# A third Strassen product in a hybrid decoder layer, with three smaller moves in its order

## The chip, the cores and the metric

The kernel runs on one core of a Trainium2 chip. TensorE (PE) multiplies, VectorE (DVE) and ScalarE (ACT) do elementwise work, GpSimd (POOL) does a little elementwise work and issues stores, SyncE (SP) issues loads; 16 DMA engines move the data. Each engine takes its instructions in the order in which the program wrote them. The metric is the time of one execution on the device in microseconds (us), median of several runs.

## What is computed

One layer of a decoder, 1024 tokens by 1024 channels, all float32. Cut to what matters (`@` with weights is what PE does, the rest is elementwise):

```python
u = rms_norm(h, norm1_g)
z_pool, z_lru, z_gelu, z_gate = split(u @ w_in)            # 512, 1024, 1024, 2048 columns
y_pool = causal_multiscale_pool(z_pool, pool_w) @ pool_proj
y_lru  = rglru_branch(z_lru, z_gelu, ...) @ lru_proj        # conv, two gates per head, scan, gelu
gates  = sigmoid(z_gate + b_gate)
h = h + (gates[0] * y_pool + gates[1] * y_lru) @ w_out
v = rms_norm(h, norm2_g)
g, u = split(v @ w_ffn_in)                                  # 2 x 2816 columns
h = h + (silu(g) * u) @ w_ffn_out
h = h + sigmoid(rms_norm(h, ple_norm_g) @ w_ple_gate) * (p @ w_ple_proj)
out = rms_norm(h, final_g)
```

## The kernel before

Activations lie transposed: a tile is 128 channels (partitions) by 1024 tokens, 512 KB, and a low and a high half mean tokens 0 to 511 and 512 to 1023. To keep float32 precision each operand is split into a high part (a cast on ACT, `hi`, L113) and a low part (a subtraction on DVE, `lo`, L117), and each product takes three matmuls of 512 columns (`mm3`, L217 to L219; `mm6`, L225, is the same for a plain product over both halves).

The stages run one after the other: p @ w_ple_proj ("PLE", first), w_in, pool_proj, lru_proj, w_out, w_fin (w_ffn_in), w_fout (w_ffn_out), the gate of the PLE term, and the last norm. w_in, w_fin and w_fout use Strassen's algorithm (`strassen`), seven products where a plain one takes eight. A pair of weight tiles (A11 to A22) and a pair of activation tiles (B11 to B22) make 2x2 blocks. `PairOf` forms the sums of weights on DVE (L192). `Acts` forms the activation operands B11, T1, T2, B21, B22, T3, T4, with subtractions on DVE (L396 to L402) that overwrite their source tiles. A unit is one product q of one pair: 12 matmuls in one PSUM bank over four tile pairs. The products come in the order 1, 5, 6, 2, 3, 7, 4, and for each the two or three pairs of a group. `Plain` and `Gated` take a bank's content into the results (copies on ACT, additions on DVE), and the bank of a pair is kept over several products.

`drive` (L274) writes the order. For each unit it does the previous unit's rest (post), loads, casts and subtracts of the weights three ahead, the unit's own preparation, some steps of background work worth half the unit's time, and then the unit's matmuls. Background generators are a queue of which the first two are looked at; `yield None` means "not in this unit any more". Into that queue go the chains of the recurrence (`chain`, L614, with two gate products per head), pooling with its products, the softplus of the recurrence's parameter, and, in w_fin, the finished tiles' operands for w_fout, which are stored to DRAM (`hidden_ops`). Units that a generator puts into `inserted` are emitted before the next unit.

Around the change: w_lru's tiles come in `done_lru`, which multiplies by a gate, adds, and splits the tile (names g and m). w_out is a plain product (L225) over eight tiles. `done_out` adds it to x (tile xr, L898), stores h, adds h squared to ss (L324), and scales h in place by gain and reciprocal norm (L902). Operands of w_fin begin in it. w_fout runs in three chunks of 3, 4 and 4 tile pairs (`CHUNKS`), and each reads its seven kinds of operands back from DRAM: `Loaded.make` (L1009) issues all tiles of one kind at once, on SP, behind or ahead of weights (L146) as the program has them. `Residual` adds the chunks' banks to h (L1031) and, in the second, the stored h (tile hr, L1022).

## Time and profile before

| | us |
|---|---|
| runs, median of three | 1447.88 (1447.34 to 1450.69) |
| profiled execution | 1451.7 |
| its span, first to last instruction | 1450.0 |
| PE busy | 1383.5 (95%), 6006 matmuls |
| DVE busy | 1033.6 (71%) |
| ACT busy | 673.7 (46%) |
| POOL busy | 90.5 (6%) |
| granted TensorE clock, mean | 0.973 of full |

Busy time is time in which an engine executes; the rest is waiting. A matmul's end is modelled: one of 512 columns shows .39 us and issues every .23 us, so a busy PE can still be paced by its issue. Shares over the whole span mix stages with different limits, so a stage is read by its own window. A clock of 1.00 is 2.4 GHz, 0.50 is 1.2 GHz. In lists of waits "A <- B" says that A's engine sat idle until B ended.

### The profile page before, as it was taken

Reading aid. Unit: us, or ns where it says so; the run is one execution under the profiler, and the core shown is the slowest. Engines: PE = TensorE matmul, PEld = TensorE weight load, DVE = VectorE, ACT = ScalarE, POOL = GpSimd, SP = SyncE. Lnnn points to the kernel's source line nnn. Section 1 sums busy time; section 2 is a strip of 40 time slices with the busy share of each in tenths; the row PEclk is TensorE's granted clock in tenths of the full one; section 3 lists DMA queues with packets and bytes.
Section 4 is the critical chain, followed back from the end, with each engine's and each line's share of the span. In section 5 each row is a group of like instructions: output and inputs, shape, how many; then the busy total and the mean of one; then the engine's idle time right before and its main releaser. Section 6 shows DMA issues by size and latency. Waiting matters only on the chain.

```text
span 1450.0 us, 16454 instructions
## 1 busy us (share of the span) xinstructions
PE 1383.5 (95%) x6006; PEld 1133.5 (78%) x6006; DVE 1033.6 (71%) x1523; ACT 673.7 (46%) x1072; POOL 90.5 (6%) x194
## 2 busy tenths in 40 slices
PE   6899999999999999999899999999999889998986
PEld 4677887877887888888788888888888678886865
DVE  3887778778865454367798888888778667767465
ACT  5468584877876021223554444444444322235231
POOL 2200010010000000000001000101010100000000
PEclk8799999999999999999999999999999999999987
DMA  7222233332558323231124344344584997703203
GB/s 276 102 79 89 78 119 121 103 114 88 217 183 336 110 87 138 86 119 65 45 90 141 139 154 158 146 160 148 217 338 174 365 356 295 297 30 116 63 25 116
DMA packets 65025, 220.55 MB, mean 152 GB/s; under 512 B 7344, under 2 KB 9904, under 8 KB 64944
## 3 DMA queue, kind: packets, MB, share of 16 engines
q1 hardware_dynamic: 46224, 151.80, 29.7%
q0 software_dynamic: 18576, 67.64, 11.6%
q8 instruction: 47, 0.77, 0.2%
q14 instruction: 34, 0.28, 0.1%
q10 hardware_dynamic: 144, 0.06, 0.0%
HBM read 147.65 MB, written 71.83 MB: 151 GB/s over the span
## 4 chain that ended last, share of the span: by engine, by line
PE 58%; issue 8%; DVE 7%; DMA 3%; ACT 2%; POOL 0%; DVEq 0%; SPq 0%; POOLq 0%; ACTq 0%
PE ps L217 16%; PE ps L218 16%; PE ps L219 16%; PE ps L225 9%; DVE w L117 1%; DMA fT<-fT 1%; DMA fB<-fB 1%; DMA wr<-w_fout 1%; DVE wr L192 1%; PE ps L363 1%; DVE pg L1106 0%; ACT w L113 0%; ACT pg L1104 0%; DVE h L1107 0%; ACT sq L1112 0%
## 5 line engine op out<-in xcount | busy, mean ns | idle before, releaser
L113 ACT CAST w<-wr 128x512 fp32r<-128x512 f32 (+2 forms) x376 | 220.6, 608 | 339.3 <-DVE wr L192 179.4
L117 DVE TENSOR_TENSOR w<-wr,w 128x512 fp32r<-128x512 f32 (+2 forms) x376 | 250.1, 672 | 66.4 <-ACT w L113 64.7
L218 PE MATMUL ps<-xT,w 128*128 128x512 f32 x640 | 251.9, 394 | 5.6 <-DVE xT L117 5.6
L217 PE MATMUL ps<-xT,w 128*128 128x512 f32 x640 | 251.9, 394 | 4.6 <-DVE z L491 4.3
L219 PE MATMUL ps<-xT,w 128*128 128x512 f32 x640 | 251.2, 392 | 0.0
L218 PE MATMUL ps<-xB,w 128*128 128x512 f32 x480 | 188.4, 392 | 1.6 <-DVE xB L117 1.5
L217 PE MATMUL ps<-xB,w 128*128 128x512 f32 x480 | 187.8, 391 | 1.6 <-ACT xB L113 1.6
L219 PE MATMUL ps<-xB,w 128*128 128x512 f32 x480 | 187.8, 391 | 0.0
L218 PEld LDWEIGHTS ps<-xT,w 128*128 128x128 f32 x640 | 121.6, 190 | 31.9 <-DVE xT L117 6.8
L217 PEld LDWEIGHTS ps<-xT,w 128*128 128x128 f32 x640 | 121.5, 190 | 32.0 <-issue 3.5
L219 PEld LDWEIGHTS ps<-xT,w 128*128 128x128 f32 x640 | 121.6, 190 | 25.8 <-DVE w L117 0.2
L218 PEld LDWEIGHTS ps<-xB,w 128*128 128x128 f32 x480 | 90.7, 189 | 21.8 <-DVE xB L117 3.1
L217 PEld LDWEIGHTS ps<-xB,w 128*128 128x128 f32 x480 | 90.8, 189 | 21.2 <-ACT xB L113 2.0
L219 PEld LDWEIGHTS ps<-xB,w 128*128 128x128 f32 x480 | 90.8, 189 | 18.8
L225 PE MATMUL ps<-m,w 128*128 128x512 f32 x384 | 87.3, 389 | 0.0
L225 PE MATMUL ps<-y,w 128*128 128x512 f32 x384 | 87.2, 389 | 0.0
L217 PE MATMUL ps<-fT,w 128*128 128x512 f32 x176 | 71.0, 403 | 15.2 <-DVE h L1031 13.0
L225 PEld LDWEIGHTS ps<-y,w 128*128 128x128 f32 x384 | 72.1, 188 | 15.0
L225 PEld LDWEIGHTS ps<-m,w 128*128 128x128 f32 x384 | 72.0, 188 | 14.9
L1031 DVE TENSOR_TENSOR h<-h,ps 128x512 f32<-128x512 f32 x68 | 46.6, 685 | 39.8 <-PE ps L219 39.3
L192 DVE TENSOR_TENSOR wr<-wr 128x512 f32<-128x512 f32 (+1 forms) x104 | 70.5, 679 | 6.0 <-DMA wr<-w_fout 3.9
L218 PE MATMUL ps<-fT,w 128*128 128x512 f32 x176 | 70.2, 399 | 0.0
(209 smaller groups left out, 2200.7 us busy)
## 6 DMA issues: line engine op xcount, KB each, us to landing
wr<-w_fin SPq DMA_DIRECT2D x44, 512.0 KB, 5.6
fT<-xT POOLq DMA_DIRECT2D x44, 512.0 KB, 6.0
fT<-fT SPq DMA_DIRECT2D x44, 512.0 KB, 9.1
wr<-w_in SPq DMA_DIRECT2D x36, 512.0 KB, 4.0
fB<-xB POOLq DMA_DIRECT2D x33, 512.0 KB, 5.4
fB<-fB SPq DMA_DIRECT2D x33, 512.0 KB, 8.3
g<-z POOLq DMA_DIRECT2D x16, 512.0 KB, 3.9
g<-g SPq DMA_DIRECT2D x16, 512.0 KB, 5.6
```

The lines of the kernel that those rows point to most:

```text
L113: act.copy(op[:, :x.shape[1]], x)
L117: dve.tensor_tensor(op[:, H:H + n], x, op[:, :n].bitcast(F32), ALU.subtract)
L192: f(self.place(out), self.place(a), self.place(b))
L217: pe.matmul(bank, a, xop[:, :H], start=first, stop=False, skip_group_check=more)
L218: pe.matmul(bank, a, xop[:, H:], start=False, stop=False, skip_group_check=more)
L219: pe.matmul(bank, b, xop[:, :H], start=False, stop=last, skip_group_check=more)
L225: pe.matmul(bank, w, xop[:, s], start=f, stop=e)
L363: pe.matmul(bank[:, i * P:(i + 1) * P], r[:, b + i:b + i + 1].broadcast_to([P, P]), ident, start=True, stop=True)
L1031: dve.tensor_add(h[t][:, s], h[t][:, s], bank)
```

## The change

1. **w_out by Strassen.** `done_lru` no longer splits its tiles; neighbouring tiles (even a, odd b) are a pair of `ma`. For each pair a background generator (`some_operands`) makes B11, T1, T2 and B21; `prepare(ma)` makes what is left within w_out. w_out runs in two groups of two pairs. `Plain` collects each result in a tile z, and `residual` adds it to x, stores h, writes the scaled tile into its own tile v, and adds the square. The pairs of v are neighbours too, and the host puts the rows of w_out and w_fin in that order.
2. **Softplus** begins when the first group of w_in has its operands ("xa").
3. **Gate and pooling products** are put in after a `yield None`.
4. **The chunks' operands** are loaded one by one by `load_some`, which each unit of the chunk's first group and of the group before calls: from the fourth unit on (the first chunk from the fifth), one for each .8 units (1.1 in the first chunk). `hidden_ops` becomes `kept_operands`, and the wait for "va" moves to `Gated.last`.

```diff
@@ -455,6 +455,15 @@
             units.extend(unit(i + j, q, where, j, size) for q in QS for j in range(size))
             i += size
+    def some_operands(acts, k, names):
+        for name in names:
+            acts.run(name, k, 0)
+            yield {"T1": 0.7, "T2": 1.4, "T4": 0.7}.get(name, 0.1)
+            yield None
+            acts.run(name, k, 1)
+            yield 0.7
...
@@ -585,6 +594,8 @@
     e_, d_, s_, s2, acc, mx, nsp, psp = (sc[:, i, :] for i in range(8))
     def softplus():
+        while "xa" not in have:
+            yield None
         lam = cv[:, C_LAM:C_LAM + NH]
         act.activation(e_, lam, AF.Abs)
...
+    def kept_operands(a, b, out, k, key):
+        acts = Acts(1)
+        acts.a[0], acts.b[0] = a, b
+        for name in ORDER:
+            acts.run(name, 0, 0)
+            yield {"T1": 0.7, "T2": 1.4, "T4": 0.7}.get(name, 0.1)
+            yield None
+            acts.run(name, 0, 1)
+            store(out[name, k], acts.op.pop((name, 0)).bitcast(F32))
+            yield 0.7
+        have.add((key, k))
+    class Loaded:
+        def __init__(self, src, key, k0, n, order, begin, step):
+            self.src, self.key, self.k0, self.op = src, key, k0, {}
+            self.order, self.begin, self.step, self.units = order, begin, step, 0
+        def load_some(self, every=False):
+            n = len(self.order) if every else int((self.units - self.begin) / self.step) + 1
+            self.units += 1
+            for name, k in self.order[len(self.op):max(n, 0)]:
+                force((self.key, self.k0 + k))
+                self.op[name, k] = at("l" + name, F32R)
+                nc.sync.dma_start(self.op[name, k].bitcast(F32), self.src[name, self.k0 + k])
...
@@ -656,6 +695,7 @@
                 have.add(("rg", c, h))
             return Unit([], emit, post)
+        yield None
         inserted.append(half(0))
         yield None
         inserted.append(half(1))
@@ -732,8 +772,9 @@
             store(m_spill[gi], mx_)
             have.add(("mx", gi))
+        yield None
         inserted.append(Unit([], emit, post))
-        yield 0.5
+        yield 0.1
...
-    ms = {}
+    ma = Acts()
...
         for b, s in zip(banks, (LOW, HIGH)):
             dve.tensor_mul(g[:, s], g[:, s], b)
         dve.tensor_add(g, g, t0.pop(m))
-        ms[m] = split(g, "m")
+        if m % 2 == 0:
+            ma.a[m // 2] = g
+        else:
+            ma.b[m // 2] = g
+            background.append(some_operands(ma, m // 2, ORDER[:4]))
     plain([w_lru[m] for m in range(KD)], KD, lambda: ys, done_lru, pre_lru, 2)
...
-    def pre_out(m, a):
-        if a == 0:
-            if m == 0:
-                state["ss2"] = at("ss")
-                state["rep1"] = norm1.spread()
-                load_xr(0)
-            if m + 1 < KD:
-                load_xr(m + 1)
-    def done_out(m, banks):
-        h = xr.pop(m)
-        for b, s in zip(banks, (LOW, HIGH)):
-            dve.tensor_add(h[:, s], h[:, s], b)
-        store(h_spill[m], h)
-        add_square(h, state["ss2"], m == 0)
-        dve.scalar_tensor_tensor(h, h, col(C_G2, m), state["rep1"], ALU.mult, ALU.mult)
-        if m < 4:
-            va.a[m] = h
-        else:
-            va.b[m - 4] = h
-        if m == 3:
-            va.make("B11")
-        if m == 4:
-            va.make("T1")
-        if m >= 4:
-            va.run("T2", m - 4, 0)
-        if m >= 5:
-            va.run("T2", m - 5, 1)
-        if m == KD - 1:
-            state["norm2"] = Rstd(state["ss2"])
-    plain([w_out[m] for m in range(KD)], KD, lambda: ms, done_out, pre_out, 2)
+    prepare_m = prepare(ma)
+    def loads_of_group(m0):
+        def pre(q, j, size):
+            i = QS.index(q)
+            if m0 == 0:
+                if i == 0 and j == 0:
+                    state["ss2"] = at("ss")
+                    state["rep1"] = norm1.spread()
+                prepare_m(q, j, size)
+            if j == 0 and i in (2, 3, 4, 5):
+                load_xr(m0 + {2: 0, 3: 2, 4: 1, 5: 3}[i])
+        return pre
+    def residual(m):
+        def then(z):
+            h = xr.pop(m)
+            dve.tensor_add(h, h, z)
+            store(h_spill[m], h)
+            v = at("v")
+            dve.scalar_tensor_tensor(v, h, col(C_G2, m), state["rep1"], ALU.mult, ALU.mult)
+            if m % 2 == 0:
+                va.a[m // 2] = v
+                if m // 2 >= 2:
+                    va.run("B11", m // 2, 0)
+            else:
+                va.b[m // 2] = v
+                if m // 2 < 2:
+                    background.append(some_operands(va, m // 2, ORDER[:3]))
+            add_square(h, state["ss2"], m == 0)
+            if m // 2 >= 2:
+                va.run("B11", m // 2, 1)
+            if m == KD - 1:
+                state["norm2"] = Rstd(state["ss2"])
+        return then
+    strassen(ma, [(w_out[2 * i], w_out[2 * i + 1]) for i in range(KD // 2)],
+             lambda i: Plain(residual(2 * i), residual(2 * i + 1)), loads_of_group(0),
+             last=loads_of_group(4), groups=[2, 2])
...
@@ -963,6 +1015,8 @@
                 background.append(self.last())
         def last(self):
+            while "va" not in have:
+                yield None
             rep, g, u = state["rep2"], self.g, self.u
             dve.tensor_mul(g, g, rep)
...
             if self.j % 2:
-                background.append(hidden_ops(self.j // 2))
+                k = self.j // 2
+                background.append(kept_operands(f_tile.pop(2 * k), f_tile.pop(2 * k + 1), f_spill, k, "f"))
...
-        def __init__(self, k0, n):
-            self.k0, self.n, self.op = k0, n, {}
-        def make(self, name):
-            for k in range(self.n):
-                self.op[name, k] = at("f" + name, F32R)
-                nc.sync.dma_start(self.op[name, k].bitcast(F32), f_spill[name, self.k0 + k])
...
-    chunks = [Loaded(k0, k1 - k0) for k0, k1 in CHUNKS]
+    chunks = [Loaded(f_spill, "f", k0, k1 - k0, [(n, k) for n in ORDER for k in range(k1 - k0)],
+                     4 if k0 == 0 else 3, 1.1 if k0 == 0 else 0.8) for k0, k1 in CHUNKS]
     def next_chunk(c):
         def last(q, j, size):
-            if c == len(CHUNKS):
-                if q == QS[3]:
-                    have.add("room")
-                if "room" in have and complete:
-                    done_fout(complete.popleft())
+            if c < len(CHUNKS):
+                chunks[c].load_some()
                 return
-            if j:
-                return
-            if q == QS[1]:
-                force(*[("f", k) for k in range(CHUNKS[c][1])])
-            if q != QS[0]:
-                chunks[c].make(ORDER[QS.index(q) - 1])
+            if q == QS[3]:
+                have.add("room")
+            if "room" in have and complete:
+                done_fout(complete.popleft())
         return last
...
     for c, (k0, k1) in enumerate(CHUNKS):
         def pre_fout(q, j, size, c=c):
-            if q == QS[0] and j == 0:
-                chunks[c].make(ORDER[-1])
+            chunks[c].load_some()
...
+    def pairs(w):
+        return w.reshape(KD // 2, 2, P, -1).transpose(1, 0, 2, 3).reshape(D, -1)
...
-        "w_out": tiles(a["w_out"][0]),
-        "w_fin": tiles(a["w_ffn_in"][0]),
+        "w_out": tiles(pairs(a["w_out"][0])),
+        "w_fin": tiles(pairs(a["w_ffn_in"][0])),
         "w_fout": tiles(a["w_ffn_out"][0].reshape(NJ, P, D)[blocks].reshape(DFF, D)),
```

DVE at the change from product 7 to product 4 of w_out's first group in the new program, and in the old one a stretch inside w_out between two output tiles (xT_ are operands, z the collected product, g the input tiles, w and wr weights). Old:

```order
L117 TENSOR_TENSOR w<-wr,w 128x512 x2
L898 TENSOR_TENSOR xr<-xr,ps 128x512 x2
L324 TENSOR_TENSOR ss<-ss,sq 128x1024
L902 SCALAR_TENSOR_TENSOR xr<-xr,cv,rstd 128x1024
L399 TENSOR_TENSOR xr<-xr 128x512
L400 TENSOR_TENSOR xr<-xr 128x512
L117 TENSOR_TENSOR xT_4861<-xr,xT_4861 128x512
L117 TENSOR_TENSOR w<-wr,w 128x512 x2
```

New:

```order
L117 TENSOR_TENSOR xT_4683<-g,xT_4683 128x512
L117 TENSOR_TENSOR xT_4711<-g,xT_4711 128x512
L496 TENSOR_TENSOR z<-z,ps 128x512
L948 TENSOR_TENSOR xr<-xr,z 128x1024
L952 SCALAR_TENSOR_TENSOR v<-xr,cv,rstd 128x1024
L324 TENSOR_TENSOR ss<-ss,sq 128x1024
L117 TENSOR_TENSOR w<-wr,w 128x512
L402 TENSOR_TENSOR g<-g 128x512 x2
L117 TENSOR_TENSOR xT_4741<-g,xT_4741 128x512
L402 TENSOR_TENSOR g<-g 128x512
L500 TENSOR_TENSOR z<-z,ps 128x512
L117 TENSOR_TENSOR w<-wr,w 128x512
```

Where one output tile stood as two additions, a square's sum and a scaling, two tiles' residual work now stands between the operands T3, the subtractions and casts of T4, and the addition that frees the bank of product 4.

SP at the second chunk of w_fout (fB_, fT_, lB_, lT_ are operands of w_fout in DRAM and in SBUF, wr weights). Old, behind eight more operands in a row:

```order
L1009 DMA fT_8734<-fT_5_282 128x1024
L1009 DMA fT_8736<-fT_6_283 128x1024
L146 DMA wr<-w_fout 128x1024
L1009 DMA fB_8770<-fB_3_291 128x1024
L1009 DMA fB_8772<-fB_4_292 128x1024
L1009 DMA fB_8774<-fB_5_293 128x1024
L1009 DMA fB_8776<-fB_6_294 128x1024
L146 DMA wr<-w_fout 128x1024 x2
```

New:

```order
L645 DMA lB_8810<-fB_6_261 128x1024
L645 DMA lT_8826<-fT_3_269 128x1024
L645 DMA lT_8828<-fT_4_270 128x1024
L146 DMA wr<-w_fout 128x1024
L645 DMA lT_8848<-fT_5_271 128x1024
L146 DMA wr<-w_fout 128x1024
L645 DMA lT_8865<-fT_6_272 128x1024
L146 DMA wr<-w_fout 128x1024
L645 DMA lT_8882<-fT_3_280 128x1024
L146 DMA wr<-w_fout 128x1024
```

The weights moved from behind blocks of four or more operands to places between single ones.

PE at the first gate product of the recurrence (xc is its operand, xB and xT are operands of w_in). Old:

```order
L218 MATMUL ps<-xB_609,w 128x512
L219 MATMUL ps<-xB_609,w 128x512
L217 MATMUL ps<-xc_1064,wrgo 128x512
L218 MATMUL ps<-xc_1064,wrgo 128x512
L219 MATMUL ps<-xc_1064,wrgo 128x512
```

New:

```order
L218 MATMUL ps<-xT_616,w 128x512
L219 MATMUL ps<-xT_616,w 128x512
L217 MATMUL ps<-xc_1064,wrgo 128x512
L218 MATMUL ps<-xc_1064,wrgo 128x512
L219 MATMUL ps<-xc_1064,wrgo 128x512
```

The gate product moved 24 matmuls back, behind two more units of w_in.

## Rows read from the trace of the kernel before

**Rows 1.** The page's busy time, share of span and instructions:

```profile
PE 1383.5 (95%) x6006; PEld 1133.5 (78%) x6006; DVE 1033.6 (71%) x1523; ACT 673.7 (46%) x1072; POOL 90.5 (6%) x194
```

**Rows 2.** Waits of PE, engine and line waited for: us, times, longest:

```profile
PE ps L217 <- DVE h L1031: 13.0, 2, 7.9
PE ps L341 <- POOL sc L598: 6.7, 1, 6.7
```

**Rows 3.** Windows: length; PE, PEld, DVE, ACT, POOL busy; clock, DMA share, GB/s:

```profile
579.40:668.30 88.90, 88.90 (x402) 73.90 (x401) 50.56 (x68) 23.82 (x37) 3.72 (x7) 1.00 0.31 107
668.30:701.00 32.70, 28.30 (x123) 23.13 (x122) 23.49 (x42) 15.01 (x26) 0.53 (x1) 0.90 0.04 17
579.40:701.00 121.60, 117.20 (x523) 97.03 (x522) 74.06 (x109) 38.83 (x63) 4.26 (x8) 0.97 0.24 83
691.01:697.84 6.83, 4.55 (x11) 3.58 (x12) 5.51 (x10) 5.70 (x11) 0.00 (x0) 0.50 0.00 0
```

**Rows 4.** DVE's groups from 579.4 to 701: busy us, mean ns, idle before:

```profile
L117 DVE TENSOR_TENSOR w<-wr,w 128x512 fp32r<-128x512 f32 x23 | 15.3, 686 | 2.8 <-ACT w L113 2.7
L902 DVE SCALAR_TENSOR_TENSOR xr<-xr,cv,rstd 128x1024 f32<-128x1024 f32 x8 | 10.3, 1285 | 11.9 <-DMA h<-xr 11.9
...
L324 DVE TENSOR_TENSOR ss<-ss,sq 128x1024 f32<-128x1024 f32 x7 | 8.6, 1225 | 8.0 <-ACT sq L323 8.0
```

**Rows 5.** Timeline, start and length in us, of w_out's and w_fin's starts:

```profile
579.40 1.28 DVE L871 TENSOR_TENSOR g<-g,ps 128x512 f32<-128x512 f32 x2 [5.15 <-PE ps L225]
...
579.42 1.95 PE L363 MATMUL ps<-ident,sm 128*128 128x128 f32 x16
...
582.63 1.29 DVE L117 TENSOR_TENSOR m<-g,m 128x512 fp32r<-128x512 f32 x2 [0.69 <-ACT m L113]
...
693.29 0.79 PE L218 MATMUL ps<-xT,w 128*128 128x512 f32 x1 [4.40 <-DVE xT L117]
```

**Rows 6.** Timeline of PE at gate and pooling products, and a window behind:

```profile
121.36 0.50 PE L217 MATMUL ps<-xc,wrgo 128*128 128x512 f32 x1 [0.62 <-ACT xc L113]
122.80 0.50 PE L218 MATMUL ps<-xc,wrgo 128*128 128x512 f32 x1 [0.94 <-DVE xc L117]
...
217.27 1.02 PE L225 MATMUL ps<-pl,wpo 128*128 128x512 f32 x2 [0.53 <-ACT pl L113]
220.55 2.25 PE L225 MATMUL ps<-pl,wpo 128*128 128x512 f32 x4 [2.25 <-DVE pl L117]
...
332.19 1.56 PE L225 MATMUL ps<-pl,wpo 128*128 128x512 f32 x4 [0.34 <-DVE pl L117]
...
219.97:226.80 6.83, 6.25 (x14) 4.74 (x15) 6.80 (x8) 5.26 (x8) 0.63 (x2) 0.50 0.31 119
```

**Rows 7.** Timeline and windows at the second chunk of w_fout:

```profile
1140.19 5.94 SPq L1009 DMA_DIRECT2D fT<-fT  x8
...
1159.89 0.62 ACT L113 CAST w<-wr 128x512 fp32r<-128x512 f32 x1 [13.06 <-DMA wr<-w_fout]
...
1161.98 0.77 PE L217 MATMUL ps<-fT,w 128*128 128x512 f32 x1 [7.94 <-DVE h L1031]
...
1175.80 0.50 PE L217 MATMUL ps<-fT,w 128*128 128x512 f32 x1 [1.70 <-ACT w L113]
...
1140.00:1160.00 20.00, 14.04 (x62) 11.28 (x61) 7.15 (x13) 3.48 (x8) 0.53 (x1) 0.97 1.02 417
1158.63:1165.46 6.83, 3.48 (x8) 2.81 (x9) 1.29 (x2) 0.62 (x1) 0.00 (x0) 0.50 1.02 419
```

**Rows 8.** Timeline of ACT, DVE and POOL in the first stage:

```profile
23.62 0.20 ACT L589 ACTIVATE sc<-cv 128x8 f32<-128x8 f32 x1
...
34.60 2.56 DVE L324 TENSOR_TENSOR ss<-ss,sq 128x1024 f32<-128x1024 f32 x2 [0.31 <-ACT sq L323]
...
30.24 1.25 POOL L598 TENSOR_TENSOR sc<-sc 128x8 f32<-128x8 f32 x1
31.57 0.23 POOL L599 TENSOR_SCALAR sc<-sc 128x8 f32<-128x8 f32 x1
```

More of the change, by code (lines that the diff above doesn't have):

```diff
@@ L981, in hybrid_block @@
                for n in ORDER for k in range(NJ // 2)}
-    def hidden_ops(k):
-        while "va" not in have:
-            yield None
-        acts = Acts(1)
-        acts.a[0], acts.b[0] = f_tile.pop(2 * k), f_tile.pop(2 * k + 1)
-        for name in ORDER:
-            acts.run(name, 0, 0)
-            yield {"T1": 0.7, "T2": 1.4, "T4": 0.7}.get(name, 0.1)
-            yield None
-            acts.run(name, 0, 1)
-            store(f_spill[name, k], acts.op.pop((name, 0)).bitcast(F32))
-            yield 0.7
-        have.add(("f", k))
-    hs, v2 = {}, {}
-    class Loaded:
-        def __init__(self, k0, n):
-            self.k0, self.n, self.op = k0, n, {}
-        def make(self, name):
-            for k in range(self.n):
-                self.op[name, k] = at("f" + name, F32R)
-                nc.sync.dma_start(self.op[name, k].bitcast(F32), f_spill[name, self.k0 + k])
+    hs, v2 = {}, {}
     class Residual:
```

## The prediction

> **What bounds the kernel now.** I read the busy table first: TensorE (PE) is busy 95% of the span, VectorE (DVE) 71% [rows 1]. So a change gains either by matmuls taken away or by PE's waits taken away. The list of PE's waits comes next [rows 2]. Its largest entries are 13.0 us in two waits at the feed-forward output and 6.7 us in the first stage; none is near the 66.5 us that PE is idle in all, so the rest is many small ones. The stretch that the change rewrites, w_out and the first nine units of w_fin, was read by windows [rows 3]. In w_out itself PE never waits (88.90 of 88.90 us), and DVE is busy only 50.56 us. In the 32.7 us behind it PE loses 4.4 us and the granted clock is 0.90. Every stretch is weighed by the engine that is late in it.
>
> The unit price is .227 us for a matmul with 512 columns: 88.90 us less 1.7 us for the 16 small matmuls ahead of them (1.95 us as shown [rows 5], less some .25 us of the last one's modelled end), over 384. A Strassen unit of 12 takes 2.72 us. DVE's prices: .605 us for 128x512 in a row (two take 1.28 us [rows 5], one alone .69) and 1.22 us for 128x1024 [rows 4].
>
> **The change part by part.**
>
> *w_out by Strassen.* PE does 28 units of 12, 336 matmuls for 384: 48 x .227 = 10.9 us less. If PE alone counted, the stretch from the end of w_lru (T0, 579.40) to the ninth unit of w_fin would hold 1.7 us of small matmuls, 28 x 2.72 = 76.2 us, 9 x 2.72 = 24.5 us and 1.7 us for the second set of small ones: 104.1 us. Before it took 122.0 us: 1.7 + 87.2 + 24.5 + 1.7, a wait of 4.4 + .16 (a matmul shows .39 us but issues every .227), and half a clock over 4.55 us of PE work, 2.3 us [rows 3, 5]. So 17.9 us are there to be had.
>
> But DVE gets more work in that shorter stretch. Counted in its order, T0 to the last row that w_fin's third operand (T2) needs: 149 instructions where before there were 109. By the prices they are 117 x .605 = 70.8 us, 24 x 1.22 = 29.3 us and 8 small ones at .2 us: 101.7 us, against 74.06 us before [rows 3]. (Before's 109 rows by the same prices give 72.3 us, so the prices fit.) What is new: subtractions of whole weight tiles, sums of two products in z, the residual added from z, three operands still split within the stage. DVE thus has as much to do as PE, and its order is fixed, so each unit whose operand or bank stands behind a long run of DVE work waits. I went through the order unit by unit:
> - The first unit wants the high half of the last tile's operand, which on ScalarE stands behind a weight cast and two copies. Before, the last lru tile was cast by 582.63 [rows 5], under the small matmuls. About 2.8 us.
> - Between the end of the ninth unit and the q4 unit of pair 0 stand the rows shown in the DVE excerpt with those just ahead of it: 12 of 512 and 5 of 1024, 7.3 + 6.1 = 13.4 us. PE has three units to do meanwhile, 8.16 us. It waits 5.3 us, and .8 us more for the rest of T4.
> - In the second group: a weight low half behind two tiles' h, v and ss, 3.4 us; banks held by ScalarE's copies, 1.9 us; then the same place as above, 15.3 us of DVE work against 8.16 us, 7.2 us.
> - Start of w_fin: its T1 4.7 us, T2 (the table load for the square root, which before cost the 4.4 us) 2.1 us.
>
> Sum 28.2 us, so 104.1 + 28.2 = 132.3 us where 122.0 us were; a clock drop behind these waits would give DVE time, so of it I add only a part, .7 us. **+11 us.** Bounds: -17.9 us (DVE never late) and -6.4 us (late only up to the first q4 unit); above, all waits and half a clock of 2.3 us [rows 3] behind each of the three long ones, +17 us. The scaling's wait for the store of h, 11.9 us of DVE's idle time [rows 4], goes with the own tile v; DVE had slack there, so PE gains nothing by it. I take +11, since each term comes from a fixed order; the end that speaks against it is w_out before, where DVE had slack everywhere.
>
> *Softplus later.* In the first stage PE waits 6.7 us, put down to a POOL step of softplus [rows 2]. Yet DVE is adding squares until 37.2, and ScalarE works back to back from 23.1; softplus holds ScalarE for two steps of .2 us only [rows 8]. PE's next instruction needs those sums, so the label names a bystander: **-.4 us**, between 0 and -6.9. If POOL's chain was the releaser, it is all 6.9.
> One thing shows on POOL: its 8-element steps take 1.25 us in places, while DVE adds 1024 columns, and .23 us in others [rows 8]. The Trainium skill, page "SBUF — State Buffer", section "Who interferes with whom", says that a DVE instruction with two SBUF inputs and a GpSimd instruction that reads SBUF contend for one interface, held for the whole instruction; the two lengths agree. By that rule softplus in w_in, where DVE has more such work, would hold POOL longer and the stores queued on it with it. That changes nothing in the sum as long as PE waits for no store there.
>
> *Gate and pooling matmuls one unit later.* Their operands are cast and split by ScalarE and DVE just before; one unit more of other matmuls, 2.72 us, lies between making and use (the first gate as a whole stands 24 matmuls later). PE's waits that this covers [rows 6]: .62 + .94 us at the first gate, .53 + 2.25 us at the second pooling unit, .34 us at the fourth, .16 us more for each, and half a clock after the second, 6.25 / 2 = 3.1 us: **-8.6 us**. The longest, 2.25 us, is below a unit; but what DVE does in that unit comes first in its queue, so the range is -12 (smaller waits too) to +2 us (they move and one grows).
>
> *Chunk operands one by one.* At the second chunk of w_fout SP issues its operand loads in blocks, eight at 1140.19, and weights behind them. DMA moves 417 GB/s at a share of 1.02, ScalarE waits 13.06 us for a weight, and PE 7.94 us behind it; 1.70 us follow later, and half a clock over 3.48 us of work [rows 7]: 7.94 + 1.70 + 2 x .16 + 1.74 = 11.7 us. In the new order a weight stands behind one or two operands, not four or twelve, and loading begins in the last group of the chunk before, at its fourth unit. Up to the chunk's first unit some 15 operands and 4 weights fall into 11 units of 9 matmuls, 22.5 us: 10 MB, 443 GB/s, a little over what the DMA moved at its fullest. So the loads are late by one or two, but only the first four and one weight are wanted at once. **-10.5 us**, from -12 to -3 us (the late load is a weight). That single loads wait one by one for free tiles puts SP at risk (rival C).
> The Trainium skill, page "DMA: Bandwidth & Descriptors", section "Issuing engines are not separate DMA queues", holds that DMAs of all engines end on the same 16; the 417 GB/s with loads from SP and stores from POOL agree. Spreading the loads then gains only by the earlier start.
>
> Sum: +11 - .4 - 8.6 - 10.5 = -8.5 us. Against the profiled execution (1451.7 us, span 1450.0) that is 1443.2 us; that execution lies 3.8 us above the median of the runs, 1447.88, so I forecast **1439 us** (A), own range 1432 to 1446.
>
> **The rivals.**
> - B: DVE does not bind, so the Strassen gain arrives. For it: DVE has 101.7 us of work and PE 104.1, so with enough slack each could run beside the other. Against: the order lets nothing overtake. With -6.4 in place of +11 it is 1422 us; with -17.9, 1410 us. The Trainium skill, page "Perfetto Trace Analysis", section "Identifying the Most-Contended Engine", advises to improve the engine with the highest occupancy first (for TensorE by weight loads too). PE at 95% agrees for the whole span; that rule would have this rival come true.
> - D: PE's small waits only move. In w_in DVE sets the pace at those places (2.25 us behind a DVE split), and a unit later it is as late. Without the -8.6 it is 1448 us: no change.
> - C: slower. SP issues in order. A single operand load that waits for a free tile holds the weight behind it, and PE waits as now in [rows 7]. If the second chunk keeps its wait and one other chunk gets one like it (7.94 + 1.70 + .2 = 9.8 us), the chunk part is +9.8 in place of -10.5: 1460 us. It is slower than before once the chunk part gives back less than 2 us.
>
> **How the numbers follow.** A .44, B .25, D .16, C .15. A measurement of this kernel can tell about 0.3% from no change, 4.3 us, so same is 1443.5 to 1452.2. Faster: A .42 and B .25; same: .02 of A and D, less .01 that falls above; slower: C and that .01. The range leaves out most of C and the lower end of B (.06): 1417 to 1454.
>
> **What would show it.** In the new trace: PE idle in w_out before the q4 units of pair 0 and pair 2 with DVE as releaser (5 and 7 us), DVE busy near 100 us in the stretch up to T2, and the stretch near 133 us. No entry of 7.9 us at the h addition of w_fout and no ScalarE wait of 13 us for a weight. No pooling wait above 1 us. The wait at the first normalization still about 6.7 us, under another name. A w_out stretch below 116 us would make the ledger wrong (B); an SP load that waits with weights behind it while PE stands, C.

## The result, and the profile after

The changed kernel takes 1462.55 us (median of four, 1461.08 to 1463.13) where the kernel before took 1448.41 in the same comparison: ratio 1.0094, 95% interval 1.0077 to 1.0111. It is slower by .9%, and outside the range that was given. The profiled execution has a span of 1461.1 us, 11.1 above before's.

By stage. The bounds are the starts of the first stage's last product, of pool_proj's first matmul, of w_lru's last matmul, and of the first matmuls of w_fout and of the PLE gate:

| us | before | after | difference |
|---|---|---|---|
| first stage, up to its last product | 51.6 | 51.4 | -.3 |
| w_in | 397.2 | 400.4 | +3.2 |
| pool_proj, lru_proj | 130.3 | 130.3 | 0 |
| w_out and w_fin | 518.5 | 534.5 | +16.0 |
| w_fout | 230.7 | 223.2 | -7.5 |
| the rest | 121.6 | 121.4 | -.2 |

All of the 16 us lie between the end of w_lru and the second spreading of a norm in w_fin; behind that w_fin is the same to .1 us. In w_in the profile of before is itself the slowest of five with its order (394.0 to 397.2 us, last section), so +3.2 us is the least that this row can mean. The first view is the page's busy time, after:

```profile
PE 1378.7 (94%) x5958; PEld 1125.8 (77%) x5958; DVE 1074.8 (74%) x1583; ACT 696.5 (48%) x1112; POOL 89.1 (6%) x194
```

There are 48 matmuls less than in [rows 1], and PE is busy 4.8 us less for it; the span grew all the same, so the loss is in waits and clock. Waits of PE, after (engine and line waited for: us, times, longest):

```profile
PE ps L217 <- DVE z L500: 16.4, 6, 7.3
PE ps L341 <- DVE ss L324: 8.3, 2, 8.2
PE ps L217 <- DVE h L1061: 7.6, 2, 5.0
PE ps L217 <- ACT xT L113: 6.4, 2, 4.6
```

Against [rows 2], the wait of 7.9 us at w_fout's addition is gone (13.0 became 7.6), the first stage's wait is there under another name, as forecast, and z L500, the addition that frees the bank of product 4, leads. Of its 16.4 us one wait of 7.3 lies in w_out; the other 9.1 us lie in w_in, where before waited 4.3 us for the same addition (its L491). xT L113 are operands of w_out and w_fin.

Windows (length; PE, PEld, DVE, ACT, POOL busy; clock, DMA share, GB/s), first of before, over w_in and over the stretch from w_lru's end to that second spread:

```profile
51.60:448.90 397.30, 383.22 (x1635) 310.21 (x1634) 316.59 (x431) 281.77 (x407) 28.26 (x54) 0.98 0.35 123
579.40:717.80 138.40, 134.00 (x598) 110.94 (x597) 86.36 (x128) 47.43 (x79) 4.26 (x8) 0.98 0.22 76
```

and the same of after, with the stretches at half clock in it:

```profile
51.40:451.80 400.40, 380.71 (x1635) 308.71 (x1634) 316.74 (x432) 283.26 (x410) 38.14 (x78) 0.98 0.33 120
582.30:736.70 154.40, 134.16 (x550) 106.91 (x550) 121.28 (x178) 70.35 (x121) 4.25 (x8) 0.90 0.25 89
...
588.78:592.19 3.41, 3.19 (x9) 2.48 (x9) 2.72 (x6) 1.75 (x3) 0.00 (x0) 0.50 0.02 5
626.32:633.15 6.83, 6.12 (x15) 4.81 (x16) 6.16 (x10) 2.27 (x4) 0.00 (x0) 0.50 0.15 57
674.11:684.35 10.24, 5.60 (x13) 4.46 (x14) 4.83 (x7) 3.08 (x6) 0.00 (x0) 0.50 0.11 45
698.00:708.24 10.24, 7.41 (x17) 5.01 (x16) 7.91 (x20) 6.39 (x11) 0.00 (x0) 0.50 0.01 2
```

PE is busy as long as before with 48 matmuls less: it runs 22.3 us of its work at half clock, which costs half of that, 11.2 us. DVE went from 86.36 to 121.28 us of the stretch. The waits themselves, in the timeline of after (start, length, [idle before <- releaser]):

```profile
588.31 0.50 PE L217 MATMUL ps<-xB,w 128*128 128x512 f32 x1 [1.95 <-ACT xB L113]
...
627.03 0.77 PE L217 MATMUL ps<-xT,w 128*128 128x512 f32 x1 [4.56 <-ACT xT L113]
...
678.75 0.77 PE L217 MATMUL ps<-xT,w 128*128 128x512 f32 x1 [7.27 <-DVE z L500]
...
701.27 0.79 PE L217 MATMUL ps<-xT,w 128*128 128x512 f32 x1 [1.86 <-ACT xT L113]
```

These are the places of the forecast: first unit, q4 of pair 0, q4 of pair 2, T1 of w_fin. The half clock begins .5 us behind the first wait, .7 us ahead of the second's end, and 2.6 us into the third; the fourth stretch begins 1.4 us ahead of the wait that ends at 701.27, behind the sums of the norm (L341). By the matmuls' starts all waits of the stretch come to 22.5 us, where before had 4.6. So the stretch adds up: 10.9 us of matmuls less, 17.9 us of waits more, and 8.9 us of half clock more (11.2 against 2.3 in before) make 15.9 of the 16.0 us.

### The profile page after: what moved, and what is told of

It is laid out like the page before. It is cut to its first block, busy times and chain, and to the rows that moved or that the text cites. A ratio compares the mean times of both kernels' runs of the same rounds, so it can differ in the third digit from the quotient of the medians.

```text
span 1461.1 us, 16476 instructions
## 1 busy us (share of the span) xinstructions
PE 1378.7 (94%) x5958; PEld 1125.8 (77%) x5958; DVE 1074.8 (74%) x1583; ACT 696.5 (48%) x1112; POOL 89.1 (6%) x194
## 4 chain that ended last, share of the span: by engine, by line
PE 45%; DVE 4%; DMA 1%; ACT 1%; issue 1%; DVEq 0%; ACTq 0%
PE ps L217 14%; PE ps L219 14%; PE ps L218 14%; PE ps L225 2%; DMA wr<-w_fout 1%; DVE w L117 1%; DMA lT<-fT 1%; DVE pg L1132 1%; DVE h L1133 0%; ACT pg L1130 0%; DVE ss L324 0%; PE ps L363 0%; ACT sq L1138 0%; DVE pg L1129 0%; DVE h L1146 0%
## 5 line engine op out<-in xcount | busy, mean ns | idle before, releaser
L113 ACT CAST w<-wr 128x512 fp32r<-128x512 f32 (+2 forms) x384 | 226.2, 608 | 353.0 <-DVE wr L192 187.0
L117 DVE TENSOR_TENSOR w<-wr,w 128x512 fp32r<-128x512 f32 (+2 forms) x384 | 256.5, 672 | 67.6 <-ACT w L113 65.8
L217 PE MATMUL ps<-xT,w 128*128 128x512 f32 x704 | 279.6, 397 | 24.3 <-DVE z L500 16.4
L218 PE MATMUL ps<-xT,w 128*128 128x512 f32 x704 | 278.5, 396 | 4.3 <-DVE xT L117 4.3
L219 PE MATMUL ps<-xT,w 128*128 128x512 f32 x704 | 278.0, 395 | 1.5 <-DVE w L117 1.5
L217 PE MATMUL ps<-xB,w 128*128 128x512 f32 x528 | 207.5, 393 | 4.6 <-ACT xB L113 3.2
L218 PE MATMUL ps<-xB,w 128*128 128x512 f32 x528 | 207.6, 393 | 2.1 <-DVE xB L117 2.1
L219 PE MATMUL ps<-xB,w 128*128 128x512 f32 x528 | 206.8, 392 | 0.0
L217 PEld LDWEIGHTS ps<-xT,w 128*128 128x128 f32 x704 | 134.5, 191 | 57.0 <-issue 16.0
L218 PEld LDWEIGHTS ps<-xT,w 128*128 128x128 f32 x704 | 134.7, 191 | 33.9 <-DVE xT L117 6.0
L219 PEld LDWEIGHTS ps<-xT,w 128*128 128x128 f32 x704 | 134.6, 191 | 30.8 <-DVE w L117 2.4
L217 PEld LDWEIGHTS ps<-xB,w 128*128 128x128 f32 x528 | 100.1, 190 | 27.5 <-ACT xB L113 4.1
L218 PEld LDWEIGHTS ps<-xB,w 128*128 128x128 f32 x528 | 100.0, 189 | 24.4 <-DVE xB L117 3.9
L219 PEld LDWEIGHTS ps<-xB,w 128*128 128x128 f32 x528 | 100.1, 190 | 20.8
L217 PE MATMUL ps<-lT,w 128*128 128x512 f32 x176 | 70.2, 399 | 8.9 <-DVE h L1061 7.6
L192 DVE TENSOR_TENSOR wr<-wr 128x512 f32<-128x512 f32 (+1 forms) x112 | 76.0, 679 | 3.1 <-DMA wr<-w_fout 1.1
L219 PE MATMUL ps<-lT,w 128*128 128x512 f32 x176 | 69.9, 397 | 0.0
L218 PE MATMUL ps<-lT,w 128*128 128x512 f32 x176 | 69.8, 397 | 0.0
L113 ACT CAST w<-s 128x512 fp32r<-128x512 f32 (+1 forms) x56 | 34.3, 613 | 55.3 <-DVE s L192 53.9
```

The source lines that it names most:

```text
L113: act.copy(op[:, :x.shape[1]], x)
L117: dve.tensor_tensor(op[:, H:H + n], x, op[:, :n].bitcast(F32), ALU.subtract)
L192: f(self.place(out), self.place(a), self.place(b))
L217: pe.matmul(bank, a, xop[:, :H], start=first, stop=False, skip_group_check=more)
L218: pe.matmul(bank, a, xop[:, H:], start=False, stop=False, skip_group_check=more)
L219: pe.matmul(bank, b, xop[:, :H], start=False, stop=last, skip_group_check=more)
```

## The experiments

"Alone" means that one part of the change was put into the kernel before. Ratios are to the kernel before, run beside each.

**Each part alone.** `e_out` is part 1, `e_gate` part 3, `e_sp` part 2, `e_loads` part 4, as in the change's diff.

> The kernel before with the Strassen w_out alone. Theory (w_out's DVE order makes PE wait, and the half clock behind the waits costs as much again): the stretch from the last w_lru matmul to w_fin's second spread is 16 us longer than before, the whole 1464 us, and w_in is as before. Rival (the longer stretch comes from something that the other parts bring, such as the moved wait for the norm's operands): the stretch is within 5 us of before's, the whole near 1450 us.

Measured: 1461.98 us, ratio 1.0098 (1.0080 to 1.0117). w_out and w_fin 534.1 us, 15.7 more than before; in the stretch 22.4 us of waits, 30.7 us at half clock, each at the place where after has it. The theory holds: nothing of it comes from other parts.

> The kernel before with the later gate and pooling products alone. Theory (they shift background work in front of the additions that free w_in's banks): w_in 3 us longer than before, the whole 1451 us. Rival (the later softplus is what shifts the background work; the later products do what was forecast): w_in 8.6 us shorter, the whole 1440 us.

Measured: 1439.37 us, .9941 (.9924 to .9957), 8.8 us faster; w_in 386.7 us. The rival holds.

> The kernel before with the later softplus alone. Theory (a bystander in the first stage): the wait before the first norm still ends within .7 us of where it did, the whole 1447.5 to 1448.5 us. Rival (it shifts the whole background queue of w_in): the whole moves by 3 us or more, w_in's waits lie elsewhere.

Measured: 1457.38 us, 1.0069 (1.0047 to 1.0090), **9.2 us slower**, w_in 406.3 us. The first stage is no worse, so the wait there had another cause, as forecast; the loss is in w_in. PE's longest waits in w_in, kernel with the later softplus alone:

```profile
PE ps L217 <- DVE z L491: 11.7, 4, 5.8
PE ps L225 <- ACT pl L113: 3.0, 1, 3.0
```

> The kernel before with the chunk operands loaded one by one alone. Theory: w_fout 7.5 us shorter as in the changed kernel, the whole 1441 us; the 8 us wait at the second chunk is gone and one of some 3 us comes later. Rival (the gain in the changed kernel came from a w_fin shifted against its stores): within 3 us of before, 1446 to 1449 us.

Measured: 1440.47 us, .9950 (.9933 to .9967), 7.7 us faster; w_fout 222.7 us. The theory holds.

**Why a later softplus costs 9 us.** `e_slot` leaves softplus where it was, and puts an empty generator into the queue:

```diff
+    def slot():
+        while "xa" not in have:
+            yield None
+        yield None
+        yield 0.4
...
     background.append(softplus())
+    background.append(slot())
```

> The kernel before, softplus where it was, and an empty generator in the background queue that waits for the first group's operands and then counts as much as softplus does: the order of w_in's gates, chains and pooling is then that of the kernel with the later softplus, without its instructions there. Theory (the place in the queue shifts the background work of all of w_in; softplus's own instructions cost nothing there): 1457 us, w_in's waits at the places of the kernel with the later softplus (6 us at 296, 3 us at 218). Rival (softplus's GpSimd steps, held up by VectorE, and its table load delay the chains): within 2 us of before, 1448 us.

Measured: 1455.56 us, 1.0066 (1.0049 to 1.0083), 9.3 us slower. Its order on PE is that of `e_sp` row by row, on DVE and ACT too but for softplus's own rows and one table load. So softplus's instructions cost nothing there, its place in the queue does. The background chains of w_in are then interleaved otherwise for the rest of the stage. One place, the timeline of DVE in `e_slot`, and PE behind it:

```profile
291.06 0.69 DVE L117 TENSOR_TENSOR w<-wr,w 128x512 fp32r<-128x512 f32 x1 [0.27 <-ACT w L113]
296.00 1.23 DVE L675 TENSOR_TENSOR ig<-ig,xc 128x1024 f32<-128x1024 f32 x1 [4.26 <-ACT ig L661]
297.15 1.22 DVE L688 TENSOR_TENSOR ig<-ig,th 128x1024 f32<-128x1024 f32 x1
298.40 2.29 DVE L690 TENSOR_TENSOR_SCAN ig<-r,ig 128x1024 f32<-128x1024 f32 x1
300.61 0.66 DVE L491 TENSOR_TENSOR z<-z,ps 128x512 f32<-128x512 f32 x1
...
301.41 0.77 PE L217 MATMUL ps<-xT,w 128*128 128x512 f32 x1 [5.83 <-DVE z L491]
```

The addition L491 frees PE's bank. It stands behind three rows of a recurrence chain (L675 to L690) whose first waits 4.26 us for ACT. In the kernel before, the last two rows of the same chain stand one addition earlier, ahead of the one at 290.18, for which PE waits .93 us. For the next one, at 291.36, which is the addition of 300.61 above, PE does not wait. Timeline of before:

```profile
286.71 1.23 DVE L682 TENSOR_TENSOR ig<-ig,th 128x1024 f32<-128x1024 f32 x1 [1.76 <-POOL th L676]
287.97 2.29 DVE L684 TENSOR_TENSOR_SCAN ig<-r,ig 128x1024 f32<-128x1024 f32 x1
290.18 0.66 DVE L491 TENSOR_TENSOR z<-z,ps 128x512 f32<-128x512 f32 x1
...
291.36 0.68 DVE L491 TENSOR_TENSOR z<-z,ps 128x512 f32<-128x512 f32 x1
...
290.99 0.47 PE L217 MATMUL ps<-xT,w 128*128 128x512 f32 x1 [0.93 <-DVE z L491]
```

**Do the later gates gain by the forecast's mechanism?** `e_gateonly` has the `yield None` before the gate products alone, `e_poolonly` that before the pooling products and the smaller cost behind it.

> The kernel before with the later gate products alone, pooling as it was. By the forecast's terms only the first gate's waits go (1.9 us of 8.6): 1446 us. Rival (any shift in the background queue changes all of w_in): 4 us or more away from that, either way.

Measured: 1446.04 us, .9991 (.9981 to 1.0001), 1.6 us less in the median. The forecast's number for this part came, but the interval does not exclude no change.

> The kernel before with the later pooling products alone (and their smaller cost in the queue). By the forecast's terms the waits at the second and fourth pooling products and the half clock behind go: 6.7 us, 1441 us. Rival (any shift in the background queue changes all of w_in): 4 us or more away from that, either way.

Measured: 1450.37 us, 1.0023 (1.0014 to 1.0033), 2.7 us **slower** where 6.7 us less were forecast: here the rival holds. Edits of -1.6 and +2.7 us alone give -8.8 together, so the gain is not a sum of waits that are covered. The page's window over w_in, of `e_gate`:

```profile
52.00:438.70 386.70, 375.32 (x1635) 306.51 (x1634) 315.56 (x429) 278.33 (x406) 26.43 (x52) 1.00 0.34 122
```

Waits in w_in went from 15.5 to 12.2 us only, and time at half clock from 17.1 to 3.4 us. The named waits are gone; six smaller ones behind L491 (5.9 us in all, none above 1.3) took their place, and in this execution the clock stayed full behind them: its 3.4 us at half clock lie at the start of w_in. Part of the fall from 17.1 us belongs to the execution of before, though. Four other profiles with its order of w_in (`e_out`, `e_loads`, `e_light`, `e_defer`) have 6.8, 6.8, 6.8 and 13.7 us at half clock there and take 394.0 to 396.5 us, so `e_gate` is 7.3 to 9.8 us shorter than these.

**The undo of one part.** `e_nosp` is the changed kernel with the softplus back in its early place.

> The changed kernel with the softplus back in its early place, all else as changed. Theory (softplus's place in the background queue costs w_in 9 us alone and some 14 us together with the later gate products): w_in 390 us as with the later gates alone, w_out's stretch 15.7 us longer and w_fout 8 us shorter than before, the whole 1444 to 1446 us. Rival (w_in's 3 us come from the gate products once w_out and the loads are changed too): the whole stays above 1455 us.

Measured: 1449.19 us, 1.0012 (1.0001 to 1.0023); w_in 386.7 us (390 expected), w_out and w_fin 15.8 us more than before, w_fout 8.1 us less; the median lies 3 us above what was expected. The rival falls: with the later gates, the later softplus costs 14 us of w_in (400.4 against 386.7), and some 12 us of the whole by the ratios (1.0094 against 1.0012).

**Both gains without the losses.** `e_both` is the kernel before with parts 3 and 4.

> The kernel before with the later gate and pooling products and the chunk operands loaded one by one, without the Strassen w_out and without the later softplus. Theory (the two gains, 8.8 and 7.7 us alone, lie in stages that don't touch each other): 1431.7 us. Rival (each shifts the other): above 1436 us.

Measured: **1431.83 us, .9901 (.9886 to .9916)**: faster than both kernels. The gain of 14.4 us agrees with the sum of the two parts alone, 16.5, within the intervals.

**What makes the waits in w_out?** Four versions. `e_light` takes work away from `e_out`:

```diff
-            v = at("v")
-            dve.scalar_tensor_tensor(v, h, col(C_G2, m), state["rep1"], ALU.mult, ALU.mult)
+            v = h
...
-            add_square(h, state["ss2"], m == 0)
+            if m == 0:
+                add_square(h, state["ss2"], True)
```

> The Strassen w_out alone, with the scaling of h (v is h) and seven of the eight tiles' squares left out: 8 x 1.24 + 7 x 1.2 = 18 us of VectorE's work less in that stretch; this part of the computation is left out. Theory (residual work in front of the rows that PE wants makes the waits, and the waits the half clock): the waits before the two q4 units fall from 4.7 and 7.4 us to below 1 us and below 3 us, the half clock behind them goes, the stretch up to w_fin's second spread is 12 us or more shorter than with the Strassen w_out alone. Rival (the weights' subtractions and the operands bound it, or ScalarE's copies): less than 6 us shorter.

Measured, in one execution: w_out and w_fin 510.4 us, 23.7 less than `e_out` and 8 less than the plain w_out; waits 7.4 us in all, 2.4 and .6 before the two q4 units (below 1 and below 3 were expected), half clock 3.4 us. Window and longest wait of `e_light` in the stretch:

```profile
575.80:706.30 130.50, 124.04 (x551) 101.36 (x550) 102.94 (x163) 63.40 (x114) 4.25 (x8) 0.99 0.31 106
...
PE ps L217 <- ACT xT L113: 2.3, 1, 2.3
```

Leaving out 18.3 us of DVE's work was worth 23.7 us. The residual work in front of PE's operands is the cause, and Strassen would pay if that work were not there. That DVE's amount alone does it is not shown: the seven squares are gone from ACT too, which is busy 63.40 us where after has 70.35. `e_defer` keeps the work and gives it to the queue:

```diff
     def residual(m):
         def then(z):
-            h = xr.pop(m)
...
+            background.append(rest(m, z))
...
+    def rest(m, z):
+        h = xr.pop(m)
+        dve.tensor_add(h, h, z)
+        store(h_spill[m], h)
+        yield 1.2
...
+        if q == 1 and j == 0:
+            force(*[("h", m) for m in range(KD)])
```

> The Strassen w_out alone, with the residual work of each tile (addition, store, scaling, square) given to the background queue in three steps, so that the addition that frees q4's bank and T4's subtractions stand ahead of most of it: the same instructions in another order. Theory (order, not the amount): the waits before the two q4 units fall below 2 us each, the stretch is 5 to 10 us shorter than with the Strassen w_out alone, the whole 1452 to 1457 us, some of it given back at w_fin's start. Rival (VectorE's amount of work binds): the waits move to w_fin's start, the whole stays at 1460 to 1464 us.

Measured: 1455.06 us, 1.0064 (1.0049 to 1.0079); the stretch 144.6 us, 9.5 less than `e_out`. Both are half right: the two waits before q4 shrank to 3.3 us and nothing, and one of 10.07 us stands at w_fin's first operand instead. The waiting is nearly the same (20.3 against 22.4 us), but gathered, with 17.1 us at half clock in place of 30.7.

`f_act`, on `e_nosp`, moves the scaling to ACT:

```diff
-            dve.scalar_tensor_tensor(v, h, col(C_G2, m), state["rep1"], ALU.mult, ALU.mult)
+            act.activation(v, h, AF.Copy, scale=col(C_G2, m))
```

> The changed kernel with the early softplus, and w_out's scaling moved from VectorE to ScalarE: v is h times the gain alone, the second norm's own factor then takes the place of the ratio of the two norms, and the first norm's factor is not spread in w_out any more (16 small matmuls and two copies less). VectorE loses 8 x 1.24 = 9.9 us in the stretch. Theory (the amount of VectorE work in front of the q4 units and of w_fin): the waits before q4 fall by 2 us or more each, the wait of the first unit goes, the half clock shrinks to 10 us or less, the stretch is 12 to 16 us shorter than with the Strassen w_out as it was, the whole 1429 to 1433 us. Rival (ScalarE is late instead: the scaling stands between its casts and copies): the stretch is less than 6 us shorter, the whole above 1438 us.

Measured: 1457.16 us, 1.0069 (1.0053 to 1.0086), slower than `e_nosp`; waits 25.4 us. The rival holds. The waits of PE in w_out and at w_fin's start in `f_act`:

```profile
PE ps L217 <- DVE z L500: 7.0, 1, 7.0
PE ps L217 <- ACT xT L113: 6.8, 3, 5.7
PE ps L219 <- DVE w L117: 3.1, 1, 3.1
```

ACT's casts of T4 and of weights now queue behind a scaling that waits for DVE's addition. The squares stand behind that scaling too, and DVE waits for them in its own order: 16.6 us ahead of the additions of squares in the stretch, where `e_nosp` has 3.3 us. DVE's row in `f_act`:

```profile
L324 DVE TENSOR_TENSOR ss<-ss,sq 128x1024 f32<-128x1024 f32 x7 | 8.6, 1226 | 16.6 <-ACT sq L323 16.6
```

`f_pool` also moves the seven additions of squares to GpSimd (`pool.tensor_add`), `f_plain` is the control with the plain w_out.

> As the kernel with the scaling on ScalarE, and the seven additions of squares in w_out moved from VectorE to GpSimd: 8.5 us of VectorE's work less again. Theory (VectorE's amount still binds): 4 to 8 us less than with the scaling on ScalarE alone, 1423 to 1428 us. Rival (GpSimd's additions hold up VectorE's, since both read two operands from SBUF, as 8-element steps took 1.25 us beside VectorE's additions, or they end later than the norm wants them): the same or more than with the scaling on ScalarE.

Measured: 1444.26 us, .9978 (.9966 to .9990), 13 us less than `f_act` (4 to 8 were expected), though above the forecast time, which rested on `f_act`'s. The theory holds on the sign, but its reason does not: DVE is not busy for less time. The stretches of `f_act` and of `f_pool`:

```profile
569.20:728.00 158.80, 135.93 (x534) 108.25 (x533) 111.17 (x168) 77.97 (x127) 4.25 (x8) 0.88 0.25 86
...
567.20:714.20 147.00, 130.23 (x534) 104.51 (x533) 113.65 (x161) 77.22 (x127) 21.39 (x15) 0.93 0.27 93
```

What went is DVE's wait of 16.6 us for the squares; that this made the 13 us is the likely reading, and no run takes it apart. What GpSimd took over came back on DVE: each of the seven GpSimd additions overlaps one DVE row that has both inputs in SBUF, and these seven rows take 10.7 us more than such rows do elsewhere. One of them, GpSimd first, then DVE, in `f_pool`:

```profile
651.00 2.47 POOL L963 TENSOR_TENSOR ss<-ss,sq 128x1024 f32<-128x1024 f32 x1 [2.08 <-ACT sq L962]
...
651.13 0.68 DVE L496 TENSOR_TENSOR z<-z,ps 128x512 f32<-128x512 f32 x1
651.85 2.71 DVE L945 TENSOR_TENSOR xr<-xr,z 128x1024 f32<-128x1024 f32 x1
```

The addition L945 takes 1225 ns in `e_nosp`, which has no GpSimd additions:

```profile
L946 DVE TENSOR_TENSOR xr<-xr,z 128x1024 f32<-128x1024 f32 x8 | 9.8, 1225 | 8.7 <-ACT z L502 8.5
```

> Control: the kernel with later gates and chunk loads and the plain w_out, its scaling moved to ScalarE too and the first norm's factor not spread in w_out. VectorE had slack there, so only the 16 small matmuls count: 1.7 us less than 1431.8 us, 1430 us. Rival (VectorE's slack was used up at w_fin's start): 4 us or more less.

Measured: 1432.2 us, .9892 (.9874 to .9910): no different from `e_both`, and too close to tell the 1.7 us from nothing. w_out and w_fin became 4.5 us shorter and w_fout 4.5 us longer (waits there 1 us more, half clock 10.2 us more by the records of these two executions).

`g_order`, on `e_nosp`, has the queue of `e_defer` (the last tile of a pair in group 2 done at once) and the squares' additions on GpSimd.

> The changed kernel with the early softplus; in w_out the residual work of all tiles but the last of each pair of the second group goes through the background queue, and the seven additions of squares are done by GpSimd: VectorE has 8.5 us less and the additions that free q4's bank stand further ahead; nothing is put on ScalarE. Theory (order and amount of VectorE's work both make w_out's waits): the stretch up to w_fin's second spread is shorter than with the plain w_out (138 us), the whole 1424 to 1430 us, below the kernel with the plain w_out (1431.8 us). Rival (ScalarE's casts and copies set q4's start once VectorE is lighter, as where the scaling was on ScalarE): the stretch stays above 142 us, the whole above 1436 us.

Measured: 1444.94 us, .9983 (.9973 to .9992); the stretch 149.3 us. The rival's numbers hold, not its cause: PE's longest wait is for DVE, not ACT, and it stands at w_fin's first unit. Timeline of PE, and the window of the stretch, in `g_order`:

```profile
668.99 0.80 PE L218 MATMUL ps<-xB,w 128*128 128x512 f32 x1 [6.90 <-DVE xB L117]
...
568.70:718.20 149.50, 130.93 (x550) 105.05 (x549) 127.07 (x171) 69.89 (x121) 23.05 (x15) 0.93 0.27 93
```

DVE has seven instructions less than after and is busy longer, 127.07 against 121.28 us: what GpSimd took over came back as longer rows, seven of them, 15.0 us in all. By the ratios it is still some 4 us faster than `e_nosp` (.9983 against 1.0012), so DVE's busy time alone does not set the stretch. No version with a Strassen w_out that computes everything beat the plain one: their stretches take 144.6 to 158.7 us, the plain one 138.4.

## Why the prediction was wrong

By stage the forecast was -.4, -8.6, +11 and -10.5 us (first stage, w_in, w_out with w_fin, w_fout), and -.3, +3.2, +16.0 and -7.5 came. So w_in is 11.8 us of the miss of 23 us, w_out 5.0 and w_fout 3.0; some 3 us more are that before's profiled execution lay 3.8 us above the median of its runs and after's .5 us.

**The step that failed: softplus.** It was costed at -.4 us by its instructions, and as to w_in the text asked only whether GpSimd's rows would delay stores. That a generator in the queue is also a place in it was left out. That place costs 9.3 us with nothing in it (`e_slot`), and 14 us of w_in in the changed kernel (400.4 against 386.7 in `e_nosp`). The bystander argument for the first stage was right: the wait there stayed, now put down to the squares' sum. The Trainium skill's rule on the interface shared by VectorE and GpSimd (page "SBUF — State Buffer", section "Who interferes with whom") was cited there and is not what cost the time: `e_slot` loses as much with softplus early.

**w_out: the sign and the waits right, a term mis-sized.** Forecast +11 us, measured +16.0 (122.0 to 138.0 us up to w_fin's ninth unit). The waits were forecast at 28.2 us and came to 22.5, place by place: 2.8 and 2.6 at the first unit, 6.1 and 4.7 at q4 of pair 0, 7.2 and 7.4 at q4 of pair 2, 5.3 and 2.8 between, 6.8 and 3.8 in w_fin, and 1.1 at an operand not listed. What failed is the clock: .7 us was added on the reasoning that a slow PE gives DVE time. The waits did come out some 6 us shorter, whether for that reason or not, but the half clock cost 11.2 us, 8.9 more than before's. The upper bound of +17 held it. The bound of -6.4 us does not follow from its terms: up to the first q4 unit these give -17.9 + 2.8 + 5.3 + .8 = -9.0, and rival B 1419 us in place of 1422; the outcome is far from both. The releaser at pair 0 was ACT's cast behind DVE's subtraction, not DVE's addition.

**Gates and pooling: the number right, the steps wrong.** -8.6 us forecast, -8.8 measured alone, but its parts of -1.9 and -6.7 came out as -1.6 and +2.7; that the sum came right was luck. Edits of the queue moved waits of 2 to 6 us about in w_in (`e_sp`, `e_slot`, `e_gateonly`, `e_poolonly`). This was rival D's mechanism, which did not come for the edit it was written for and came for softplus's.

**Chunk loads: right, smaller.** -10.5 us forecast, -7.7 measured. PE's wait fell from 7.94 to 2.57 us, and the weight is still late. The second chunk's first weight as SP issues it in before, then the timeline at the same place of after, for [rows 7]:

```profile
1147.14 0.33 SPq L146 DMA_DIRECT2D wr<-w_fout  x1
...
1161.35 1.01 SPq L146 DMA_DIRECT2D wr<-w_fout  x1
...
1173.35 0.62 ACT L113 CAST w<-wr 128x512 fp32r<-128x512 f32 x1 [11.41 <-DMA wr<-w_fout]
...
1175.44 0.47 PE L217 MATMUL ps<-lT,w 128*128 128x512 f32 x1 [2.57 <-DVE h L1061]
...
1160.00:1180.00 20.00, 17.43 (x70) 13.99 (x69) 9.29 (x15) 3.36 (x8) 0.53 (x1) 0.91 1.02 414
```

The DMA is as full as before (414 against 417 GB/s), so what changed is the order. Counted from w_fout's first matmul (1097.68 and 1116.57), the weight is issued at 44.8 us where before had 49.5, behind six of the chunk's operands and not twelve, and cast at 56.8 where before had 62.2. The loading as a whole does not begin earlier: the chunk's first operands are issued at 31.8 us, in before at 28.7. The Trainium skill's page "DMA: Bandwidth & Descriptors", section "Issuing engines are not separate DMA queues", was read to the effect that spread loads gain only by an earlier start; the rows agree that the DMA is no faster, and the start that is earlier is the weight's.

**The rivals.** B (DVE does not bind) fell: PE waited for operands and banks behind DVE's rows, and `e_light`, with residual work left out, shows what it would have given. Weight loads at 78% [rows 1] put TensorE ahead of DVE's 71% too, so a share over the whole span could not tell. C forecast the right time, 1460 us, for a cause that did not occur: no load stands with PE behind it as before. The measured parts alone, +13.8 - 8.8 + 9.2 - 7.7 = +6.5, fall 7.6 us short of the whole (+14.1). Some 3 us of that are softplus, which costs about 12 us on top of the other three and 9.2 alone; the rest lies between those three together (+1.9, `e_nosp`) and their sum (-2.7). With intervals of some 2.5 us either way for each part, the shortfall is not far above the noise, and what makes it is not shown.

What stays open: why a given shift of the queue lands on a good or a bad interleaving. It was measured, not derived. Nor was a place of softplus looked for that leaves the queue as it is.

## What to carry to other kernels

Where a queue with credits writes the order, an edit of any member is an edit of everything behind it: read the new order on the engine that frees PE's buffers, and measure each such edit alone and with the others. Matmuls taken away gained nothing here, where another engine has as much to do in the shortened stretch; count that engine's rows in order against PE's units, and price each long wait with the half clock behind it (11 us for 22 us of waits here). A change of four parts can hide two good ones: without the other two, the later gates and the single loads made the fastest version, 1431.8 us.

## What the runs showed of the hardware

One order of w_in, with the same waits to .1 us from 77 us of the span on, spent 10.2 us of that part at half clock in one execution (before) and 3.4 in another (`e_out`); w_in took 397.2 and 394.0 us, though the second has one wait of 1.4 us more at its start. `e_loads` and `e_light` took 394.1 us with this order, `e_defer` 396.5. One place is the window behind the pooling waits [rows 6], 6.83 us at half clock in before. In `e_out`, whose w_in has the same order, it is half as long:

```profile
220.30:223.71 3.41, 3.41 (x8) 2.45 (x9) 3.41 (x6) 3.38 (x6) 0.10 (x1) 0.50 0.28 113
```

The other place is the wait of 2.9 us for z L491 that ends at 441.7 in before: of the five profiles only before's has half clock behind it, 3.4 us. So two profiles of one order can differ by 3 us in a stage for no reason in the order.

GpSimd's addition of 128x1024 took 2.35 to 2.50 us in `f_pool`, about twice VectorE's 1.22. Each of the seven overlaps one VectorE row with both inputs in SBUF, and that row ended .55 us (512 columns) or 1.08 us (1024 columns) after GpSimd's addition, as if it had begun only then; rows with an input in PSUM took their usual .68 us beside it. So three of the eight additions L945 took 2.09 to 2.90 us and the other five 1.22 us: the contention that [rows 8] shows on GpSimd works both ways. The Trainium skill's page "SBUF — State Buffer", section "Who interferes with whom", holds that a VectorE instruction with two SBUF inputs contends with a GpSimd instruction that reads SBUF, and one with at most one such input does not; the rows agree.
